# A weighted sum of two expert outputs: ten tiles of 13 or 12 tokens in place of eleven of 12 or 10

## The chip, the cores and the metric

The kernel runs on one core of one Trainium2 chip. The metric is the device time of one execution in microseconds (us); the median of three runs of the kernel before is 239.36 us (239.26 to 239.48). The core's VectorE (DVE), ScalarE (ACT) and SyncE (SP) are used; TensorE does nothing here and GpSimd (POOL) only sets a few constants. Data goes between the device's memory (HBM) and the core's on-chip memory (SBUF, 128 partitions) by DMA transfers, which SP and ACT issue from their own instruction streams, each into a queue of its own (q1 of the profile is SP's, q10 is ACT's). Sixteen DMA engines serve both queues.

## The reference

For each of 16 x 1024 = 16,384 tokens there are two rows of 512 float32 values (the outputs of two experts) and two weights; the result is the weighted sum of the two rows.

```python
def setup_inputs():
    batch, seq, hidden, n_experts, k = 16, 1024, 512, 8, 2
    return {
        "expert_outputs": np.random.randn(batch, seq, k, hidden).astype(np.float32),
        "combine_weights": np.random.randn(batch, seq, k).astype(np.float32),
    }

def reference(expert_outputs, combine_weights):
    weights = combine_weights[..., np.newaxis]
    return np.sum(expert_outputs * weights, axis=2).astype(np.float32)
```

So 64 MiB come in, 128 KiB of weights come in, and 32 MiB go out. There are 3 x 512 arithmetic operations a token.

## The kernel before

Each of the 128 partitions takes 128 tokens. One token is 4 KB of input (its two rows lie side by side) and 2 KB of output, so a tile of c tokens on all partitions is c x 512 KB of input, in 128 contiguous rows of c x 4 KB, one for a partition, and c x 256 KB of output, in 128 rows of c x 2 KB.

Which tokens belong to which partition is settled in two regions (`rows`, lines 40 to 44). The first `main` = 10 tokens of every partition come from the first 1,280 tokens of the input, and the other `LAST` = 118 from the rest. Inside a region a partition's tokens are contiguous, so from one partition's row to the next the input steps by 40 KB in the first region and by 118 x 4 KB = 472 KB in the second; the output steps by half of that.

The work is cut into 11 tiles (`TILES`, line 30) of 10, 12 (nine times) and 10 tokens. Four rooms of 12 tokens each lie in one SBUF tile, `et`; tile g is loaded into room g % 4, is worked on there in place, and its result is put into the first half of the same room. In what follows ln is the load of tile n, sn the store of its results, w0 the first transfer of weights and w1 the second.

The order on each engine is the order of the program (`tc.manual_schedule`); only waits for data hold an instruction up.

- SP issues the loads (`load`, line 71): first l0 in two transfers, of 2 and 8 tokens (the 2 tokens in pieces of 4 KB), and l1, l2 and l3. From then on l(g+4) is issued when sg has landed, because it overwrites the room that sg reads. SP also issues the last two stores.
- ACT issues, at the start, a small store of zeros ahead of everything (line 104, 16 pieces of 512 B, overwritten later by s0), then w0 (10 tokens' weights) and w1 (118 tokens' weights), and then the stores s0 to s6 (line 121).
- DVE multiplies a whole tile by its weights in one instruction (line 83), then adds its two halves in another (line 90). This holds for tiles 0 to 8 (`WHOLE`).
- Tile 9 (`MIXED`) shares the work: ACT multiplies the first expert's rows, one instruction a token (line 87), DVE the second expert's in one instruction (line 89), and DVE adds (line 90).
- Tile 10 goes token by token: ACT multiplies the first expert's row (line 95), DVE multiplies the second and adds the first (line 96).
- The results of tiles 7 and 8 leave as one store of 24 tokens (48 KB rows), those of tiles 9 and 10 as one of 22 tokens (44 KB rows); both stores are issued by SP.

Of the kernel before, what the change touches and what calls it, by code (L numbers as in the profile page):

```python
# [1 line left out]

# [4 lines left out]


@with_exitstack
def kernel(  # L10
    ctx: ExitStack,
    tc: tile.TileContext,
    expert_outputs: bass.AP,
    combine_weights: bass.AP,
    out: bass.AP,
):

    nc = tc.nc
    b, s, k, h = expert_outputs.shape
    assert k == 2
    n = b * s
    P = nc.NUM_PARTITIONS
    per = n // P
    assert per * P == n

    ROOM, ROOMS = 12, 4
    TILES = [10, 12, 12, 12, 12, 12, 12, 12, 12, 12, 10]  # L30
    FIRST = [2, 8, 12, 12, 12]
    STORES = [[0], [1], [2], [3], [4], [5], [6], [7, 8], [9, 10]]
    WHOLE = [0, 1, 2, 3, 4, 5, 6, 7, 8]
    MIXED = [9]
    LAST = 118
    assert sum(TILES) == per and [g for st in STORES for g in st] == list(range(len(TILES)))
    main = per - LAST
    starts = [sum(TILES[:g]) for g in range(len(TILES))]

    def rows(x):  # L40

        first = x[0 : P * main, :].rearrange("(p t) f -> p t f", p=P)
        second = x[P * main : n, :].rearrange("(p t) f -> p t f", p=P)
        return lambda t, c: first[:, t : t + c, :] if t < main else second[:, t - main : t - main + c, :]

    flat = out.rearrange("b s h -> (b s) h")
    eo = rows(expert_outputs.rearrange("b s k h -> (b s) (k h)"))
    cw = rows(combine_weights.rearrange("b s k -> (b s) k"))
    o = rows(flat)

    dt = mybir.dt.float32
    mult = mybir.AluOpType.mult
    add = mybir.AluOpType.add
    copy = mybir.ActivationFunctionType.Copy

    pool = ctx.enter_context(tc.tile_pool(name="all", bufs=1))
    et = pool.tile([P, ROOMS * ROOM, k * h], dt)
    halves = et.rearrange("p j (k h) -> p (j k) h", k=k)
    wt = pool.tile([P, per * k], dt)
    wk = wt.rearrange("p (t k) -> p t k", k=k)  # L60
    zt = pool.tile([16, 128], dt)
    warm = pool.tile([P, 1], dt)

    def place(t):
        g = max(g for g in range(len(TILES)) if starts[g] <= t)
        return g % ROOMS * ROOM + t - starts[g]

    def load(t, c, **kw):
        at = place(t)
        assert place(t + c - 1) == at + c - 1  # L70
        nc.sync.dma_start(out=et[:, at : at + c], in_=eo(t, c), **kw)  # L71

    def weights(q, t, c):
        q.dma_start(out=wk[:, t : t + c, :], in_=cw(t, c))

    def combine(g, base):
        at, c, t0 = g % ROOMS * ROOM, TILES[g], starts[g]
        if g in WHOLE or g in MIXED:
            room = halves[:, k * at : k * (at + c), :]
            x0, x1 = et[:, at : at + c, 0:h], et[:, at : at + c, h : 2 * h]  # L80
            if g in WHOLE:
                wb = wt[:, k * t0 : k * (t0 + c)].unsqueeze(2).to_broadcast([P, k * c, h])
                nc.vector.tensor_tensor(out=room, in0=room, in1=wb, op=mult)  # L83
            else:
                for i in range(c):
                    x = et[:, at + i, 0:h]
                    nc.scalar.activation(out=x, in_=x, func=copy, scale=wt[:, k * (t0 + i) : k * (t0 + i) + 1])  # L87
                w1 = wk[:, t0 : t0 + c, 1:2].to_broadcast([P, c, h])
                nc.vector.tensor_tensor(out=x1, in0=x1, in1=w1, op=mult)  # L89
            nc.vector.tensor_tensor(out=halves[:, base : base + c, :], in0=x0, in1=x1, op=add)  # L90
            return
        for i in range(c):
            t = k * (t0 + i)
            x0, x1 = halves[:, k * (at + i), :], halves[:, k * (at + i) + 1, :]
            nc.scalar.activation(out=x0, in_=x0, func=copy, scale=wt[:, t : t + 1])  # L95
            nc.vector.scalar_tensor_tensor(  # L96
                out=halves[:, base + i, :], in0=x1, scalar=wt[:, t + 1 : t + 2], in1=x0, op0=mult, op1=add
            )

    with tc.manual_schedule():  # L100
        nc.vector.memset(zt, 0.0)  # L101

        ahead = flat[0 : P * main, :].rearrange("(q t) h -> q (t h)", q=16)
        nc.scalar.dma_start(out=ahead[:, 0:128], in_=zt)  # L104
        weights(nc.scalar, 0, main)
        weights(nc.scalar, main, per - main)
        nc.scalar.activation(out=warm, in_=nc.const_aps.tensor(1.0, (P, 1), dt), func=copy)  # L107

        t = 0
        for i, c in enumerate(FIRST):  # L110
            load(t, c, **({"max_dma_last_dim": k * h * 4} if i == 0 else {}))
            t += c
        assert t == sum(TILES[:ROOMS])
        for j, st in enumerate(STORES):
            base, c = st[0] % ROOMS * ROOM * k, 0
            for g in st:
                combine(g, base + c)
                c += TILES[g]
            assert c <= k * ROOM
            q = nc.sync if j in (7, 8) else nc.scalar  # L120
            q.dma_start(out=o(starts[st[0]], c), in_=halves[:, base : base + c, :])
            for g in st:
                if g + ROOMS < len(TILES):
                    load(starts[g + ROOMS], TILES[g + ROOMS])


# [1 line left out]
_INS = ['expert_outputs', 'combine_weights']  # L128
_OUTS = [((16, 1024, 512), 'float32')]


# [23 lines left out]
```

## Time and profile before

| what | value |
|---|---|
| median of 3 runs | 239.36 us (239.26 to 239.48) |
| span of the profiled execution, first to last instruction | 237.6 us |
| what lies around the span, against the median | 1.8 us |
| DVE busy | 192.1 us (81%) |
| ACT busy | 15.2 us (6%) |
| moved by DMA | 100.80 MB, 424 GB/s over the span |
| loads and weights on SP's and ACT's queues, HBM read | 67.24 MB |
| HBM written | 33.56 MB |

The profiled execution has no device time of its own on record beside its span; the median of the runs stands in for it, so 237.6 us of span and 1.8 us around it make its 239.4 us.

The page's DMA line gives, in 40 slices of the span, the share of time in which the 16 DMA engines had a packet in hand, and the line below it what they moved. A window row gives the same for a stretch that is asked for; it counts a packet where it starts, so a short stretch is blurred by the packets at its edges. The list of DMA issues gives the time from the issue of a transfer to its landing, queueing included. The waits of SP are those of its queue of DMA issues, which is not counted as busy time.

### The profile page before, as it was taken

How to read it: one execution, taken by the hardware profiler on the slowest of the kernel's cores; microseconds unless marked ns; L12 is line 12 of the kernel's file. 1: busy time of each engine (PE TensorE's matmuls, PEld its weight loads, DVE VectorE, ACT ScalarE, POOL GpSimd, SP SyncE). 2: the span in 40 equal slices, each digit the busy share in tenths (PEclk: the TensorE clock that was granted, in tenths of full speed). 3: DMA queues.
4: the chain of work that ended last, by engine and by line, in shares of the span. 5: the costliest groups of instructions: out<-in, count | busy, mean ns of one | idle time of the engine just before them, and what ended most of it. 6: DMA issues, size and time to landing. Idle time of an engine off the chain costs nothing.

```text
span 237.6 us, 154 instructions
## 1 busy us (share of the span) xinstructions
DVE 192.1 (81%) x31; ACT 15.2 (6%) x24; POOL 0.2 (0%) x4
## 2 busy tenths in 40 slices
DVE  0039999999999996998799699969987999998000
ACT  2000000000000000000000000000000008482000
POOL 0000000000000000000000000000000000000000
DMA  7999998999999999999999999999999999999895
GB/s 266 442 445 405 456 481 375 375 430 477 439 447 414 397 405 455 463 397 430 430 505 422 447 414 397 414 447 463 397 439 422 463 404 434 441 463 463 375 485 243
DMA packets 3472, 100.80 MB, mean 424 GB/s; under 512 B 512, under 2 KB 656, under 8 KB 912
## 3 DMA queue, kind: packets, MB, share of 16 engines
q1 hardware_dynamic: 2144, 79.17, 77.6%
q10 hardware_dynamic: 1328, 21.64, 21.2%
HBM read 67.24 MB, written 33.56 MB: 424 GB/s over the span
## 4 chain that ended last, share of the span: by engine, by line
DMA 60%; DVE 30%; issue 1%; DVEq 0%; ACTq 0%; SPq 0%
DMA et<-in_expert_outputs_dram 30%; DMA out_dram<-et 24%; DVE et L83 15%; DVE et L90 10%; DMA wt<-in_combine_weights_dram 6%; DVE et L89 3%; DVE et L96 3%; DVEq L150 0%; ACTq L104 0%; DVE zt L101 0%; SPq L71 0%; DVEq L96 0%; DVEq L83 0%; DVEq L90 0%
## 5 line engine op out<-in xcount | busy, mean ns | idle before, releaser
L83 DVE TENSOR_TENSOR et<-et,wt 128x12288 f32<-128x12288 f32 (+1 forms) x9 | 114.5, 12719 | 25.8 <-DMA wt<-in_combine_weights_dram 14.9
L90 DVE TENSOR_TENSOR et<-et 128x6144 f32<-128x6144 f32 (+1 forms) x10 | 64.5, 6451 | 0.4
L87 ACT ACTIVATE et<-et,wt 128x512 f32<-128x512 f32 x12 | 7.5, 709 | 193.0 <-DMA et<-in_expert_outputs_dram 193.0
L96 DVE SCALAR_TENSOR_TENSOR et<-et,wt 128x512 f32<-128x512 f32 x10 | 6.7, 747 | 0.1
L89 DVE TENSOR_TENSOR et<-et,wt 128x6144 f32<-128x6144 f32 x1 | 6.6, 6552 | 0.0
L95 ACT ACTIVATE et<-et,wt 128x512 f32<-128x512 f32 x10 | 6.2, 707 | 4.7 <-DMA et<-in_expert_outputs_dram 4.7
L107 ACT ACT_TABLE_LOAD x1 | 1.3, 1283 | 2.4 <-issue 2.4
L101 DVE MEMSET zt<- 16x128 f32 x1 | 0.2, 165 | 0.8 <-PEq L139 0.8
L107 ACT ACTIVATE warm<-const-float32-1.0 128x1 f32<-128x1 f32 x1 | 0.2, 203 | 0.0
L139 POOL MEMSET const-bfloat16-1.0<- 128x1 bf16 x1 | 0.1, 101 | 0.0
L139 POOL MEMSET const-uint8-127<- 128x1 uint8 x1 | 0.1, 101 | 0.0
L139 POOL MEMSET const-float32-0.0<- 128x1 f32 x1 | 0.1, 98 | 0.2 <-issue 0.2
L139 POOL MEMSET const-float32-1.0<- 128x1 f32 x1 | 0.1, 98 | 0.0
## 6 DMA issues: line engine op xcount, KB each, us to landing
et<-in_expert_outputs_dram SPq DMA_DIRECT2D x9, 6144.0 KB, 35.3
out_dram<-et ACTq DMA_DIRECT2D x6, 3072.0 KB, 31.9
out_dram<-et SPq DMA_DIRECT2D x1, 6144.0 KB, 24.3
out_dram<-et SPq DMA_DIRECT2D x1, 5632.0 KB, 17.6
et<-in_expert_outputs_dram SPq DMA_DIRECT2D x1, 5120.0 KB, 21.1
et<-in_expert_outputs_dram SPq DMA_DIRECT2D x1, 4096.0 KB, 14.4
out_dram<-et ACTq DMA_DIRECT2D x1, 2560.0 KB, 24.9
et<-in_expert_outputs_dram SPq DMA_DIRECT2D x1, 1024.0 KB, 5.1
```

What stands on the lines that cost most here:

```text
L83: nc.vector.tensor_tensor(out=room, in0=room, in1=wb, op=mult)
L87: nc.scalar.activation(out=x, in_=x, func=copy, scale=wt[:, k * (t0 + i) : k * (t0 + i) + 1])
L89: nc.vector.tensor_tensor(out=x1, in0=x1, in1=w1, op=mult)
L90: nc.vector.tensor_tensor(out=halves[:, base : base + c, :], in0=x0, in1=x1, op=add)
L95: nc.scalar.activation(out=x0, in_=x0, func=copy, scale=wt[:, t : t + 1])
L96: nc.vector.scalar_tensor_tensor(out=halves[:, base + i, :], in0=x1, scalar=wt[:, t + 1 : t + 2], in1=x0, op0=mult, op1=add)
L101: nc.vector.memset(zt, 0.0)
L107: nc.scalar.activation(out=warm, in_=nc.const_aps.tensor(1.0, (P, 1), dt), func=copy)
L139: nc = _bacc.Bacc("TRN2", target_bir_lowering=False, num_devices=1)
```

## The change

The four rooms hold 13, 13, 12 and 13 tokens, and there are ten tiles, of 13 tokens, except tiles 2 and 6, which have 12 and share the room of 12. The first 115 tokens of each partition make the first region (460 KB from one partition's input row to the next, 230 KB in the output), and the last 13, which are tile 9, the second (52 KB and 26 KB).

- l0 comes as 2 and 11 tokens; the other loads are whole tiles. SP issues 11 loads in place of 12, and again the last two stores.
- The weights come in three transfers in place of two, on ACT's queue: 13 tokens (w0), 102 tokens (w1), and 13 tokens for tile 9 (w2), which lie in the second region.
- Tiles 0 to 7 are done as whole tiles. Tile 8 is the mixed one: DVE multiplies the first expert's rows of its first 3 tokens in an instruction of its own, ACT those of the other 10, and DVE the second expert's rows of all 13, then adds. Tile 9 goes token by token on ACT and DVE (`pair`).
- The results of tiles 7 and 8 leave as one store of 26 tokens (52 KB rows). The results of tile 9 leave alone (26 KB rows); they are put into the room of 12, which held tile 6, and its own room is only read.

```diff
-    ROOM, ROOMS = 12, 4
-    TILES = [10, 12, 12, 12, 12, 12, 12, 12, 12, 12, 10]
-    FIRST = [2, 8, 12, 12, 12]
-    STORES = [[0], [1], [2], [3], [4], [5], [6], [7, 8], [9, 10]]
-    WHOLE = [0, 1, 2, 3, 4, 5, 6, 7, 8]
-    MIXED = [9]
-    LAST = 118
+    SIZES = [13, 13, 12, 13]
+    ROOMS = len(SIZES)
+    ROOM0 = [sum(SIZES[:r]) for r in range(ROOMS)]
+    TILES = [13, 13, 12, 13, 13, 13, 12, 13, 13, 13]
+    FIRST = [2, 11, 13, 12, 13]
+    STORES = [[0], [1], [2], [3], [4], [5], [6], [7, 8], [9]]
+    MIXED = {8: 3}
+    LAST = 115
+    N = len(TILES)
...
-        first = x[0 : P * main, :].rearrange("(p t) f -> p t f", p=P)
-        second = x[P * main : n, :].rearrange("(p t) f -> p t f", p=P)
+        first = x[0 : P * LAST, :].rearrange("(p t) f -> p t f", p=P)
+        second = x[P * LAST : n, :].rearrange("(p t) f -> p t f", p=P)
...
+        if g == N - 1:
+            for i in range(c):
+                pair(t0 + i, x0[:, i, :], x1[:, i, :], halves[:, base + i, :])
             return
...
+        if g in MIXED:
+            v = MIXED[g]
+            for i in range(v, c):
+                x = x0[:, i, :]
+                nc.scalar.activation(out=x, in_=x, func=copy, scale=wt[:, k * (t0 + i) : k * (t0 + i) + 1])
+            w0 = wk[:, t0 : t0 + v, 0:1].to_broadcast([P, v, h])
+            nc.vector.tensor_tensor(out=x0[:, 0:v, :], in0=x0[:, 0:v, :], in1=w0, op=mult)
+            w1 = wk[:, t0 : t0 + c, 1:2].to_broadcast([P, c, h])
+            nc.vector.tensor_tensor(out=x1, in0=x1, in1=w1, op=mult)
...
-        weights(nc.scalar, 0, main)
-        weights(nc.scalar, main, per - main)
+        weights(nc.scalar, 0, TILES[0])
+        weights(nc.scalar, TILES[0], LAST - TILES[0])
+        weights(nc.scalar, LAST, per - LAST)
...
+        load(0, 0, 2, max_dma_last_dim=k * h * 4)
+        load(0, 2)
+        for g in range(1, ROOMS):
+            load(g)
         for j, st in enumerate(STORES):
-            base, c = st[0] % ROOMS * ROOM * k, 0
+            base = k * ROOM0[st[0] % ROOMS if st != [N - 1] else (N - 4) % ROOMS]
+            c = 0
```

More of the change, by code (lines that the diff above doesn't have):

```diff
@@ L27 @@
     assert per * P == n
-    ROOM, ROOMS = 12, 4
-    TILES = [10, 12, 12, 12, 12, 12, 12, 12, 12, 12, 10]
-    FIRST = [2, 8, 12, 12, 12]
-    STORES = [[0], [1], [2], [3], [4], [5], [6], [7, 8], [9, 10]]
-    WHOLE = [0, 1, 2, 3, 4, 5, 6, 7, 8]
-    MIXED = [9]
-    LAST = 118
-    assert sum(TILES) == per and [g for st in STORES for g in st] == list(range(len(TILES)))
-    main = per - LAST
-    starts = [sum(TILES[:g]) for g in range(len(TILES))]
+    SIZES = [13, 13, 12, 13]
[7 more added lines that the diff above has]
+    N = len(TILES)
+    assert sum(TILES) == per
+    starts = [sum(TILES[:g]) for g in range(N)]
     def rows(x):
-        first = x[0 : P * main, :].rearrange("(p t) f -> p t f", p=P)
-        second = x[P * main : n, :].rearrange("(p t) f -> p t f", p=P)
-        return lambda t, c: first[:, t : t + c, :] if t < main else second[:, t - main : t - main + c, :]
+        first = x[0 : P * LAST, :].rearrange("(p t) f -> p t f", p=P)
+        second = x[P * LAST : n, :].rearrange("(p t) f -> p t f", p=P)
+        return lambda t, c: first[:, t : t + c, :] if t < LAST else second[:, t - LAST : t - LAST + c, :]
     flat = out.rearrange("b s h -> (b s) h")
@@ L56 @@
     pool = ctx.enter_context(tc.tile_pool(name="all", bufs=1))
-    et = pool.tile([P, ROOMS * ROOM, k * h], dt)
+    et = pool.tile([P, sum(SIZES), k * h], dt)
     halves = et.rearrange("p j (k h) -> p (j k) h", k=k)
@@ L62, with load @@
     warm = pool.tile([P, 1], dt)
[L64 to L71, printed above, removed]
+    def load(g, skip=0, c=None, **kw):
+        c = TILES[g] - skip if c is None else c
+        at = ROOM0[g % ROOMS] + skip
+        nc.sync.dma_start(out=et[:, at : at + c], in_=eo(starts[g] + skip, c), **kw)
@@ L73, in weights @@
     def weights(q, t, c):
         q.dma_start(out=wk[:, t : t + c, :], in_=cw(t, c))
-    def combine(g, base):
[L77 to L90, printed above, removed]
-            return
[L92 to L98, printed above, removed]
@@ new lines, in pair @@
+    def pair(t, x0, x1, y):
+        nc.scalar.activation(out=x0, in_=x0, func=copy, scale=wt[:, k * t : k * t + 1])
+        nc.vector.scalar_tensor_tensor(
+            out=y, in0=x1, scalar=wt[:, k * t + 1 : k * t + 2], in1=x0, op0=mult, op1=add
+        )
+    def combine(g, base):
+        at, c, t0 = ROOM0[g % ROOMS], TILES[g], starts[g]
+        room = halves[:, k * at : k * (at + c), :]
+        x0, x1 = et[:, at : at + c, 0:h], et[:, at : at + c, h : 2 * h]
+        if g == N - 1:
+            for i in range(c):
+                pair(t0 + i, x0[:, i, :], x1[:, i, :], halves[:, base + i, :])
+            return
+        if g in MIXED:
[7 more added lines that the diff above has]
+            nc.vector.tensor_tensor(out=x1, in0=x1, in1=w1, op=mult)
+        else:
+            wb = wt[:, k * t0 : k * (t0 + c)].unsqueeze(2).to_broadcast([P, k * c, h])
+            nc.vector.tensor_tensor(out=room, in0=room, in1=wb, op=mult)
+        nc.vector.tensor_tensor(out=halves[:, base : base + c, :], in0=x0, in1=x1, op=add)
@@ L100 @@
     with tc.manual_schedule():
         nc.vector.memset(zt, 0.0)
-        ahead = flat[0 : P * main, :].rearrange("(q t) h -> q (t h)", q=16)
+        ahead = flat[0 : P * LAST, :].rearrange("(q t) h -> q (t h)", q=16)
         nc.scalar.dma_start(out=ahead[:, 0:128], in_=zt)
-        weights(nc.scalar, 0, main)
-        weights(nc.scalar, main, per - main)
+        weights(nc.scalar, 0, TILES[0])
+        weights(nc.scalar, TILES[0], LAST - TILES[0])
+        weights(nc.scalar, LAST, per - LAST)
@@ L107 @@
         nc.scalar.activation(out=warm, in_=nc.const_aps.tensor(1.0, (P, 1), dt), func=copy)
[L109 to L113, printed above, removed]
+        load(0, 0, 2, max_dma_last_dim=k * h * 4)
+        load(0, 2)
+        for g in range(1, ROOMS):
+            load(g)
         for j, st in enumerate(STORES):
-            base, c = st[0] % ROOMS * ROOM * k, 0
+            base = k * ROOM0[st[0] % ROOMS if st != [N - 1] else (N - 4) % ROOMS]
+            c = 0
@@ L118 @@
                 c += TILES[g]
-            assert c <= k * ROOM
             q = nc.sync if j in (7, 8) else nc.scalar
@@ L122 @@
             for g in st:
-                if g + ROOMS < len(TILES):
-                    load(starts[g + ROOMS], TILES[g + ROOMS])
+                if g + ROOMS < N:
+                    load(g + ROOMS)
 _INS = ['expert_outputs', 'combine_weights']
```

## The prediction

> **What bounds the kernel now.** I read the page's DMA lines first, then the rate in windows cut at the landings of loads, then SP's waits, the forms of instructions, and at last the issues of transfers one by one.
>
> ```profile
> span 237.6 us, 154 instructions
> ...
> DVE 192.1 (81%) x31; ACT 15.2 (6%) x24; POOL 0.2 (0%) x4
> ...
> DMA  7999998999999999999999999999999999999895
> ...
> DMA packets 3472, 100.80 MB, mean 424 GB/s; under 512 B 512, under 2 KB 656, under 8 KB 912
> ```
>
> ```profile
> core 0: us, DVE busy (x) ACT busy (x) POOL busy (x), PEclk, DMA share, GB/s
> 0.00:1.80 1.80, 0.17 (x1) 0.00 (x0) 0.20 (x4) 1.00 0.00 0
> 15.66:30.58 14.92, 14.63 (x2) 0.00 (x0) 0.00 (x0) 1.00 1.00 430
> 30.58:70.79 40.21, 40.14 (x5) 0.00 (x0) 0.00 (x0) 1.00 0.99 418
> 92.57:179.65 87.08, 78.06 (x8) 0.00 (x0) 0.00 (x0) 1.00 1.00 434
> ```
>
> ```profile
> SPq L71 <- DMA out_dram<-et: 169.7, 7, 41.5
> ```
>
> The DMA engines are full from the first slice to the last but one. The windows say at what rate: 430 GB/s where l1 runs with w1 alone, 434 where loads and stores alternate. 100.80 MB at 434 GB/s are 232.3 us. Before the first byte lie 1.80 us (the first window), and after the last landing, at 236.8 as worked out below, 0.8 us of span. These make 234.9 of 237.6 us. Of the 2.7 us left, the window from 30.58 to 70.79 holds most: at 418 rather than 434 GB/s it loses 40.21 x (1 - 418/434) = 1.5 us, blurred by the packets at its edges. DVE is 81% busy, but its idle time and SP's 169.7 us of waits for stores are the same thing seen twice: loads wait for rooms, and rooms for stores that share the DMA engines. So bytes decide, as long as some transfer is always queued. The change moves the same bytes. It can act only through holes in the DMA, through the cost of a row or an alternation, and through the two ends.
>
> **The two ends and the first tiles.** These rows carry the schedule: issue to landing, and the times of issue.
>
> ```profile
> et<-in_expert_outputs_dram SPq DMA_DIRECT2D x1, 4096.0 KB, 14.4
> et<-in_expert_outputs_dram SPq DMA_DIRECT2D x1, 1024.0 KB, 5.1
> ```
>
> ```profile
> et<-in_expert_outputs_dram SPq DMA_DIRECT2D x1, 6144.0 KB, 28.9
> wt<-in_combine_weights_dram ACTq DMA_DIRECT2D x1, 118.0 KB, 28.9
> wt<-in_combine_weights_dram ACTq DMA_DIRECT2D x1, 10.0 KB, 14.4
> ```
>
> ```profile
> 15.92 10.83 DVE L83 TENSOR_TENSOR et<-et,wt 128x10240 f32<-128x10240 f32 x1 [14.94 <-DMA wt<-in_combine_weights_dram]
> ...
> 212.45 6.71 DVE L96 SCALAR_TENSOR_TENSOR et<-et,wt 128x512 f32<-128x512 f32 x10
> ```
>
> ```profile
> 32.30 0.35 ACTq L121 DMA_DIRECT2D out_dram<-et  x1
> ```
>
> ```profile
> 187.86 0.33 SPq L71 DMA_DIRECT2D et<-in_expert_outputs_dram  x1
> ```
>
> ```profile
> 219.19 0.34 SPq L121 DMA_DIRECT2D out_dram<-et  x1
> ```
>
> ```profile
> 199.25 20.28 SPq L121 DMA_DIRECT2D out_dram<-et  x2
> ```
>
> ```profile
> out_dram<-et SPq DMA_DIRECT2D x1, 6144.0 KB, 24.3
> out_dram<-et SPq DMA_DIRECT2D x1, 5632.0 KB, 17.6
> et<-in_expert_outputs_dram SPq DMA_DIRECT2D x1, 5120.0 KB, 21.1
> ```
>
> The last load lands at 187.86 + 21.1 = 209.0. The first of the two closing stores goes out at 199.25 and lands at 199.25 + 24.3 = 223.5, the second at 219.19 and lands at 219.19 + 17.6 = 236.8. Between these two landings 5632 KB (5.767 MB) take 13.24 us, 435 GB/s with stores alone: no hole, though the second store was issued only 223.5 - 219.2 = 4.3 us before the first had landed. That lead is the yardstick below.
>
> w1, with one row for each partition, landed 28.9 us after issue, just as long as l1 of as many rows. So the two queues take turns row by row, whatever the rows' size.
>
> **The change part by part, and its cost.** Durations for the compute come from here:
>
> ```profile
> L83 DVE TENSOR_TENSOR et<-et,wt 128x12288 f32<-128x12288 f32 x8 | 103.6, 12956 | 10.8 <-DMA et<-in_expert_outputs_dram 10.8
> L90 DVE TENSOR_TENSOR et<-et 128x6144 f32<-128x6144 f32 x9 | 59.0, 6558 | 0.4
> L87 ACT ACTIVATE et<-et,wt 128x512 f32<-128x512 f32 x12 | 7.5, 709 | 193.0 <-DMA et<-in_expert_outputs_dram 193.0
> ...
> L89 DVE TENSOR_TENSOR et<-et,wt 128x6144 f32<-128x6144 f32 x1 | 6.6, 6552 | 0.0
> ```
>
> *First tile larger (13 tokens).* l0's second part grows by 3 tokens, 1.57 MB or 3.7 us at 430 GB/s, so l0 and w0 land near 19.4 in place of 15.7 us. Tile 0 then takes DVE 13/12 x (12.96 + 6.56) = 21.1 us, and s0 goes out at 40.5 in place of 32.3. Cost: nothing, because four rooms now hold 51 tokens (26.7 MB) in place of 46, and that load alone keeps the engines busy past 61 us. From there the first stores carry on. Uncovered, the 3.7 us would count in full.
>
> *w2, a third transfer of weights.* The bytes of weights are the same 128 KB. New are 8 more rows a DMA engine, each taking a turn against a row of l2. A price for turns with such small rows: l1 with w1 is 6.412 MB, 14.73 us at the 435 GB/s of stores alone; it took 14.92, 0.19 us more. A price for turns of loads with stores: one load and one store, 9.437 MB, take 21.77 us (the 87.08 us window holds four) against 21.68 at 435: 0.09 us for 8 turns. The bounds are 0 (if the 0.19 us belong to l1 alone) and +0.2; I take +0.1, as the price in the row that mixes loads and stores and near the middle. In ACT's queue s0 stands behind w2, which lasts as long as l2, to about 51 us. So s0 starts some 8 us later than its issue, and lands near l3, at about 74 us; only then can l4 go out. At that moment SP's queue runs dry, and the DMA lives from s1 alone, issued at 40.5 + 21.1 = 61.6, with 3328 KB or 7.8 us of work. That is the cover. l4 needs only the 1.1 us that l0 needed from its issue (0.7) to the first byte (1.80). Without the cover these 1.1 us would be lost.
>
> The Trainium skill, "DMA: Bandwidth & Descriptors", section "Queues, rings and completion order", has each DMA engine change between queues only after a packet of some 9 to 17 descriptors. By that rule w2's eight rows would pass in one turn, s0 would not be held by l2, and the hole at 74 us would not even need its cover; the sum would lose the +0.1 us. The trace does not agree: w1, landing with l1 after 28.9 us, took its turns one row at a time.
>
> *One load less, rows of 52 in place of 48 KB.* SP saves one issue of 0.33 us, off the path, since SP waits 169.7 us for stores. Each engine has 8 load rows fewer; if the 0.19 us of the l1 window were the load rows' own, that would be worth up to -0.2 us. The stores s0 to s6 are seven as before, with 56 rows an engine and as many turns against loads. I take 0, bounds -0.2 and 0, since stores and loads together run within 0.4% of stores alone.
>
> *Other pitch.* The two regions of before have 40 and 472 KB. l0's second part with w0 (4106 KB from 5.8, where the 1024 KB landed, to 1.2 + 14.4 = 15.6 us) makes about 429 GB/s at 40 KB pitch, and l1 430 GB/s at 472 KB. I take 0 for 460 KB and for 52 KB; what it would cost is a rival.
>
> *The tail.* After l9 lands, what is left is s7 with s8, 6656 KB, and s9, 3328 KB: 10.22 MB at 435 GB/s, 23.5 us. With an end at 236.9, l9 lands at 213.4. l8 lands before it by l9's 6656 KB and by what is left of s6 then, some 2100 KB: 8.97 MB at 434 GB/s, so at 192.7. Tile 8 costs DVE 1536 elements, 13 x 512 and again 13 x 512, at 6552/6144 ns each: 1.6 + 7.1 + 7.1 = 15.8 us; ACT's 10 rows at 0.709 us run beside it. The store of tiles 7 and 8 goes out at 208.5, 4.9 us before l9 has landed, where 4.3 us was enough before. Tile 9: one ACT row, 0.7 us, then 13 x 0.671 = 8.7 us on DVE (212.45 row: 6.71 us for 10), so s9 goes out at 222.8; the store before it lands at 236.9 - 7.8 = 229.1, a lead of 6.3 us. Its results go to tile 6's room, whose store lands before 210: no wait. Lanes of completion semaphores used again (by l3, from the store of zeros) are free within 6 us. Cost 0.
>
> *DVE's work.* Tiles 0 to 7 hold 102 tokens at 1.626 us, 165.9; with 15.8 and 8.7 that is 190.4 against 192.1 us. Off the path, nothing.
>
> The sum: 237.6 + 0.1 = 237.7 us of span, and with the 1.8 us around it (the median of the runs, 239.36, less 237.6) 239.45 us. Its own bounds, -0.2 to +0.2 for each of two terms, give 239.1 to 239.8.
>
> **Rivals.** *Slower, a hole before the closing stores.* If the store of tiles 7 and 8 comes too late to follow l9, the DMA is idle once l9 is through. For: its lead of 4.9 us rests on an estimate of what is left of s6, and each engine sits on a row of l9 for 52 KB / 27.2 GB/s = 1.96 us. It decides where the lead falls under that row and the 1.1 us from issue to first byte, about 3 us. Against: 4.3 us sufficed before. Price: up to 1.1 us, or the 1.96 us of a row if DVE is late by that much: 240.6 to 241.4; I put it at 240.9.
>
> *Faster, the early loss goes.* The window 30.58 to 70.79 loses up to 1.5 us, at no wait that the profile shows; it is where the first store joins the loads, and the change moves that moment by 8 us. Were half of it gone, 0.75 us: 238.7. Against: the cause isn't visible, and the first store still has to join.
>
> *Slower, the pitch.* If 460 KB spreads worse over memory than 472 KB, 1% of the loads' 67 MB at 434 GB/s is 1.5 us: 241.0. Against: 40 KB and 472 KB run alike here.
>
> [...]
>
> **How the numbers follow.** My forecast, no change that can be measured, has 0.60; the early loss going 0.16; the hole 0.13; the pitch 0.07; other losses near the start 0.04. About 0.2% (0.5 us) is what a measurement of this kernel tells from no change. Faster by more: 0.16; within: 0.60; slower: 0.24. The predicted time is 239.45, with 239.1 to 239.8 as that case's own range. For 8 in 10 I reach to half the early loss and to the near end of the hole, with a little on the fast side: 238.6 to 240.6.
>
> **What would show it.** Steps right: windows of alternating loads and stores still at 434 GB/s; first multiply near 19.4; first large store issued near 40.5, and landing near 74 with SP's l4 just after it; the 26-token store issued 4 to 5 us before l9 lands; the last store issued near 222.8; DMA slices without a digit under 8 but at the ends. Wrong: a window of low rate near 74 or 213 (a hole), steady windows below 430 (pitch), or a window at 30 to 75 us at 430 or more (the early loss gone).

## The result, and the profile after

The changed kernel takes 240.71 us (median of four runs, 240.34 to 240.81), the one before 239.42 us in the same comparison: a ratio of 1.0054, with a 95% interval of 1.0040 to 1.0068. It is 1.3 us slower, where 239.45 us and no measurable change had been forecast, and just outside the range.

The page of the changed kernel, its lines on the span, DVE and the DMA:

```profile
span 239.0 us, 155 instructions
...
DVE 190.2 (80%) x33; ACT 15.8 (7%) x25; POOL 0.2 (0%) x4
...
DMA  7989999999999999999999999999999999989995
...
DMA packets 3472, 100.80 MB, mean 422 GB/s; under 512 B 640, under 2 KB 784, under 8 KB 1040
```

The same bytes, the same full DMA line, and 1.4 us more of span. So the engines were hardly ever without a packet, but somewhere a packet took longer. Windows of the changed kernel, cut at the landings of l0, l1, l3, l4 and l8, with one more for 77 to 85.2 us:

```profile
core 0: us, DVE busy (x) ACT busy (x) POOL busy (x), PEclk, DMA share, GB/s
0.00:1.80 1.80, 0.17 (x1) 0.00 (x0) 0.20 (x4) 1.00 0.00 0
19.02:34.98 15.96, 15.84 (x2) 0.00 (x0) 0.00 (x0) 1.00 1.00 429
34.98:73.74 38.76, 38.73 (x4) 0.00 (x0) 0.00 (x0) 1.00 0.98 417
73.74:103.70 29.96, 28.04 (x4) 0.00 (x0) 0.00 (x0) 1.00 1.02 426
77.00:85.20 8.20, 8.20 (x2) 0.00 (x0) 0.00 (x0) 1.00 0.99 367
103.70:196.20 92.50, 82.87 (x8) 0.00 (x0) 0.00 (x0) 1.00 1.00 434
```

Loads alone run at 429 and the steady part at 434 GB/s, as before. New is the stretch from 77 to 85 us: 367 GB/s with a DMA share of 0.99. The kernel before has a low figure there too, but with a lower share, and the two go together where packets are counted at their starts:

```profile
77.00:85.00 8.00, 7.97 (x2) 0.00 (x0) 0.00 (x0) 1.00 0.91 393
```

393 GB/s at a share of 0.91 are 432 for a full share, as in the steady part; 367 at 0.99 are only 371. The stretch belongs to what happened at 74 us, which these rows of the changed kernel show (from issue to landing for w2 and s0; times of issue for s0, l4 and the two closing stores):

```profile
wt<-in_combine_weights_dram ACTq DMA_DIRECT2D x1, 13.0 KB, 47.4
...
40.29 0.35 ACTq L122 DMA_DIRECT2D out_dram<-et  x1
...
out_dram<-et ACTq DMA_DIRECT2D x1, 3328.0 KB, 33.6
...
73.97 0.33 SPq L68 DMA_DIRECT2D et<-in_expert_outputs_dram  x1
...
212.28 0.35 SPq L122 DMA_DIRECT2D out_dram<-et  x1
...
224.21 0.34 SPq L122 DMA_DIRECT2D out_dram<-et  x1
```

s0 goes out at 40.29 and lands at 40.29 + 33.6 = 73.9, with l3 (73.74); l4 is issued at 73.97 into an empty queue. (In these rows wt is w2, 40.29 is s0, 73.97 is l4, 212.28 and 224.21 are the closing stores of 26 and of 13 tokens.)

A window counts a packet where it starts. For the rest I spread each packet of the trace evenly over its own time and asked how far the bytes moved lag behind a steady 435.2 GB/s, a yardstick near the 435 GB/s of the last store before. The lag in us at eight moments, for the profiled executions of the two kernels and six of the experiments (told below). At 236 us f4 and h1 have moved all their bytes, so their 4.37 there is only the end of the count:

```
us from start              6     30     40     60     75     85    200    236
before                  2.77   2.96   3.31   3.89   3.95   3.99   4.44   4.57
changed                 2.49   2.67   2.76   3.52   3.58   4.85   5.30   5.53
two transfers (f4)      2.51   2.66   2.72   3.39   3.44   3.48   3.92   4.37
hold put back (g2)      2.51   2.66   2.74   3.28   3.35   4.65   5.09   5.27
hold, swapped (g3)      2.61   2.76   2.87   3.31   3.37   4.72   5.16   5.36
l4 late (h1)            2.48   2.62   2.68   3.40   3.45   3.50   3.93   4.37
two ahead of s0 (e4)    2.49   2.66   2.73   2.92   3.92   3.96   4.39   4.53
before with w2 (e2)     2.72   2.93   3.02   3.21   3.67   4.05   4.51   4.62
```

The changed kernel starts 0.28 us better, is still 0.37 us ahead at 75 us, loses 1.27 us in the ten that follow, and then keeps pace. At 236 us it is 0.96 us behind; the last 0.5 us of the span lie at the end: the 16 engines complete the last store between 237.15 and 238.22 us, before the change between 236.22 and 236.77.

The packets of the changed kernel show the join of l4 (load rows of 53,248 B, store rows of 26,624 B; grouped by order of start, durations are means):

```
store rows 75.93..76.33 x16, 987 ns each
store rows 76.92..77.31 x16, 1049 ns
store rows 77.90..78.20 x12, 1184 ns
load rows  78.31..79.68 x15, 2709 ns    (1966 ns in the steady part)
...
completions of s1, one for each engine: 87.86 to 90.92
```

Four engines took l4's first row a turn before the other twelve; rows of both kinds went slow (the longest load row took 3246 ns), and from then on the engines were up to 3 us apart. Engines without a packet account for little of it: between 73.5 and 91 us all sixteen together lack 1.55 us, 0.1 us for each.

### The profile page after: what moved, and what is told of

Same layout as the page of the kernel before. It is cut to its first block, busy times and chain, and to the rows that moved or that the text cites. A ratio compares the mean times of both kernels' runs of the same rounds, so it can differ in the third digit from the quotient of the medians.

```text
span 239.0 us, 155 instructions
## 1 busy us (share of the span) xinstructions
DVE 190.2 (80%) x33; ACT 15.8 (7%) x25; POOL 0.2 (0%) x4
## 4 chain that ended last, share of the span: by engine, by line
DMA 63%; DVE 28%; issue 2%; ACT 0%; DVEq 0%; ACTq 0%; SPq 0%
DMA et<-in_expert_outputs_dram 28%; DMA out_dram<-et 27%; DVE et L98 18%; DMA wt<-in_combine_weights_dram 7%; DVE et L99 7%; DVE et L75 3%; ACT et L74 0%; DVEq L151 0%; ACTq L105 0%; DVE zt L102 0%; DVEq L98 0%; SPq L68 0%; ACTq L74 0%
## 5 line engine op out<-in xcount | busy, mean ns | idle before, releaser
L98 DVE TENSOR_TENSOR et<-et,wt 128x13312 f32<-128x13312 f32 (+1 forms) x8 | 110.1, 13756 | 27.5 <-DMA wt<-in_combine_weights_dram 18.1
L99 DVE TENSOR_TENSOR et<-et 128x6656 f32<-128x6656 f32 (+1 forms) x9 | 62.8, 6973 | 0.4
L91 ACT ACTIVATE et<-et,wt 128x512 f32<-128x512 f32 x10 | 6.2, 712 | 191.8 <-DMA et<-in_expert_outputs_dram 191.8
L75 DVE SCALAR_TENSOR_TENSOR et<-et,wt 128x512 f32<-128x512 f32 x13 | 8.7, 747 | 3.2 <-ACT et L74 3.2
L74 ACT ACTIVATE et<-et,wt 128x512 f32<-128x512 f32 x13 | 8.1, 713 | 12.2 <-DMA et<-in_expert_outputs_dram 12.2
L95 DVE TENSOR_TENSOR et<-et,wt 128x6656 f32<-128x6656 f32 x1 | 7.1, 7084 | 0.0
L93 DVE TENSOR_TENSOR et<-et,wt 128x1536 f32<-128x1536 f32 x1 | 1.8, 1759 | 2.1 <-DMA et<-in_expert_outputs_dram 2.1
```

Source lines behind the costliest of these rows:

```text
L75: nc.vector.scalar_tensor_tensor(out=y, in0=x1, scalar=wt[:, k * t + 1 : k * t + 2], in1=x0, op0=mult, op1=add)
L93: nc.vector.tensor_tensor(out=x0[:, 0:v, :], in0=x0[:, 0:v, :], in1=w0, op=mult)
```

## The experiments

Two theories stood first. A: w2, which takes its turns row by row beside l2, holds s0 back; s0 lands with l3, the load queue runs dry, and the late join of l4 costs the time. B: the rows of 52 KB, or the pitch of 460 KB, cost it.

**e1: w2 behind l3 on SP's queue.**

```diff
-        weights(nc.scalar, LAST, per - LAST)
...
             load(g)
+        weights(nc.sync, LAST, per - LAST)
```

> The changed kernel with one edit: w2 is issued by SP behind l3, no longer by ACT ahead of s0. Theory A (w2, row by row behind l2, holds s0 back; s0 lands with l3, SP's queue runs dry, and the joining of l4 at 77 to 85 us slows all engines by 1.2 us and leaves them 1 us apart at the end): s0 starts near 44 us and lands near 66 to 68, l4 is issued before l3 lands, the slow stretch at 77 to 85 us is gone, and the time falls from 240.7 by 1.2 to 1.7 us, to 239.0 to 239.5. Theory B (the rows of 52 KB or the pitch of 460 KB cost it): 240.5 to 240.9, and a slow stretch stays.

Measured: 243.81 us, ratio 1.0179 (1.0151 to 1.0206). s0 did land early, at 67.7, and l4 was issued at 67.76. But on SP's queue w2 stood ahead of l4, and each of its rows of 104 B waited for a row of s1 of 0.98 us, so l4 began only at 80.8 us. A slow stretch of 0.57 us followed when s2 joined at 83 to 91, the engines drifted apart until l8 landed between 195.9 and 200.2, and DVE, which needs all of l8, issued the store of 26 tokens at 216.33, when l9 was through:

```profile
212.50:217.00 4.50, 3.80 (x1) 0.06 (x1) 0.00 (x0) 1.00 0.11 47
```

47 GB/s for 4.5 us is the hole that the prediction had as a rival. The time missed both expectations; the experiment moved the hold from s0 to l4 and so decides neither theory.

**e2: a w2 in the kernel before.**

```diff
-        weights(nc.scalar, main, per - main)
+        weights(nc.scalar, main, 105)
+        weights(nc.scalar, main + 105, 13)
```

> The kernel before with one edit: w1's 118 tokens come in two transfers on ACT's queue, of 105 and of 13, so that 8 more rows for each engine stand ahead of s0. Theory A: s0 starts only when l2 is through (about 49 us), lands with l3 near 71, SP's queue runs dry, l4 joins late; 0.8 to 1.7 us slower than before, 240.2 to 241.1. Theory B: 0.0 to 0.2 us slower, 239.4 to 239.6.

Measured: 239.58 us, ratio 1.0007 (0.9997 to 1.0017). The schedule came out as A says: s0 landed at 66.0 with l3 at 65.8, and l4 joined at 69.7 to 70.8, six engines a turn ahead of ten. The price did not, and the time lies in the range of B: the table shows 0.84 us lost from 60 to 85, but at 60 us the kernel was 0.68 us ahead, since the stumble that costs the kernel before 0.5 us at 45 to 48 us is missing here.

**e3: the regions swapped, and so no w2.**

```diff
-        first = x[0 : P * LAST, :].rearrange("(p t) f -> p t f", p=P)
+        first = x[0 : P * HEAD, :].rearrange("(p t) f -> p t f", p=P)
...
+        weights(nc.scalar, 0, HEAD)
+        weights(nc.scalar, HEAD, per - HEAD)
```

with `HEAD = 13` in place of `LAST` throughout.

> The changed kernel with the regions the other way round: the first 13 tokens of each partition are the first region (52 KB pitch), the other 115 the second (460 KB). Two transfers of weights do (13 and 115 tokens), there is no w2. Theory A: as with w2 on SP's queue, 239.0 to 239.5; if the faster start of the changed kernel (0.28 us) came from the pitch of its first rows, it is lost here and this kernel lies 0.3 us above that one. Theory B (the pitch of 460 KB): 240.5 to 240.9.

Measured: 238.98 us, ratio 0.9985 (0.9975 to 0.9996): the same tiles, rooms, rows of 52 KB and pitch of 460 KB, a little faster than before, with 0.04 us lost from 75 to 85. B is out. The lag at 6 us is 2.67 us, between the 2.77 of before and the 2.49 of the changed kernel.

**e4: two small transfers ahead of s0.**

```diff
-        weights(nc.scalar, TILES[0], LAST - TILES[0])
+        weights(nc.scalar, TILES[0], 51)
+        weights(nc.scalar, TILES[0] + 51, 51)
```

> The changed kernel with w1 cut into two transfers of 51 tokens, so that two small transfers stand ahead of s0 and beside l2 and l3. Theory A with a fixed price of a queue that runs dry and is joined again: 240.5 to 241.0, the slow stretch moved later (s0 starts near 66 us and lands near 75 to 82). If the price grows with how long SP's queue is dry: 241.0 to 243. Theory B: 240.7 to 241.0, and the slow stretch stays at 77 to 85 us.

Measured: 239.30 us, ratio 0.9996 (0.9987 to 1.0006). All of the expectations missed. s0 waited until l3 was nearly through (66 us), the load queue ran dry for 12 us, and at 77.7 to 78.6 l4, issued at 74.21, joined without loss: 15 of 16 engines took its first row in one step, at 1966 ns a row. So a dry queue has no fixed price. The issue of l4:

```profile
74.21 0.33 SPq L68 DMA_DIRECT2D et<-in_expert_outputs_dram  x1
```

This made the second theory, A2: the join costs, by how its moment falls among the engines. Its rival C: the 13-token rooms lose the time whatever w2 does.

**f1: w2 behind s6. f4: the first region's weights in one transfer, so that two stand ahead of s0, as before the change.**

```diff
-        weights(nc.scalar, LAST, per - LAST)
...
+            if j == 6:
+                weights(nc.scalar, LAST, per - LAST)
```

```diff
-        weights(nc.scalar, 0, TILES[0])
-        weights(nc.scalar, TILES[0], LAST - TILES[0])
+        weights(nc.scalar, 0, LAST)
         weights(nc.scalar, LAST, per - LAST)
```

> The changed kernel with w2 issued by ACT behind s6, where nothing waits behind it. Theory A2 (the loss of the changed kernel lies where the loads, having run dry because w2 held s0 back, join the running store again: rows go slow there and the engines part; the moment of the join among the engines decides how much, 0 to 1.3 us): s0 lands near 68, l4 is issued before l3 lands, no slow stretch at 77 to 85 us, the last landings within 0.6 us of each other, 238.7 to 239.2. Theory C (13-token rooms lose it whatever w2 does, and the swapped regions cured it by the pitch of tile 4's rows): a slow stretch at 75 to 90 us of 0.5 us or more, 239.8 to 240.9.

> The changed kernel with the weights of the first region, 115 tokens, in one transfer, so that only two transfers stand ahead of s0, as before the change, and s0 joins beside l2. Theory A2: as with w2 last, 238.7 to 239.3. Theory C: 239.8 to 240.9.

f4 took 238.95 us, ratio 0.9982 (0.9971 to 0.9993), with no slow stretch. Its windows from l3's landing to l4's, and on to l8's, and the issues of l4 and of the store of 26 tokens:

```profile
76.55:99.94 23.39, 23.36 (x3) 0.00 (x0) 0.00 (x0) 1.00 1.00 431
99.94:192.47 92.53, 84.98 (x9) 0.00 (x0) 0.00 (x0) 1.00 1.00 433
...
67.74 0.33 SPq L68 DMA_DIRECT2D et<-in_expert_outputs_dram  x1
...
208.47 0.35 SPq L121 DMA_DIRECT2D out_dram<-et  x1
```

f1 took 243.98 us, ratio 1.0195 (1.0178 to 1.0212), outside both ranges, but lost nothing at 77 to 85 (at 200 us its lag was 3.97 us, f4's 3.92). Near the end w2's rows took turns with rows of the closing store and landed at 222.5; ACT waited for them, and the last store landed 5 us later than f4's. From the waits of f1:

```profile
ACT et L74 <- DMA wt<-in_combine_weights_dram: 24.0, 1, 24.0
```

C falls, and A2 stands so far; f1's own loss is the same row-by-row turn at a place where I had not reckoned with it.

**f5: the room of 12 second.** The edit was wrong: tile 9 with its 13 tokens then shares the room of 12, and overwrites a token of the next one, which chains the tiles. 292.43 us say nothing on the question.

```diff
-    SIZES = [13, 13, 12, 13]
+    SIZES = [13, 12, 13, 13]
...
-    TILES = [13, 13, 12, 13, 13, 13, 12, 13, 13, 13]
+    TILES = [13, 12, 13, 13, 13, 12, 13, 13, 13, 13]
```

> The changed kernel with the room of 12 second in place of third (rooms of 13, 12, 13, 13; w2 still ahead of s0). The hold and the dry queue stay, only the moment of the join moves against the engines' rows. Theory A2: s0 still lands with l3, and the loss at the join lies anywhere from 0 to 1.3 us: 239.0 to 240.8. If the loss of a dry queue were a fixed price: 240.5 to 240.9. Theory C: 240.5 to 240.9.

**f6: the kernel before with a long pitch at the start.**

```diff
-    LAST = 118
+    LAST = 22
```

> The kernel before with its first region of 106 tokens (424 KB from row to row) and the last 22 tokens, the last store's, as the second region; the weights come as 106 and 22 tokens. If the faster start of the changed kernel (0.28 us in the first 6 us) comes from a long pitch of the first rows: 0.2 to 0.4 us faster than before, 238.9 to 239.1. If it has another cause: 239.2 to 239.5.

Measured: 239.22 us, ratio 0.9996 (0.9986 to 1.0005). The lag at 6 us fell from 2.77 to 2.53 us, as in the changed kernel; the time did not follow beyond its uncertainty and lies in the range of "another cause"; in the profiled run the stumble at 45 to 48 us was 0.2 us larger.

**g2 and g3: the hold put back, into f4 and into e3.**

```diff
-        weights(nc.scalar, LAST, per - LAST)
+        weights(nc.scalar, LAST, 7)
+        weights(nc.scalar, LAST + 7, per - LAST - 7)
```

```diff
-        weights(nc.scalar, HEAD, per - HEAD)
+        weights(nc.scalar, HEAD, 102)
+        weights(nc.scalar, HEAD + 102, 13)
```

> The kernel with two transfers of weights (115 and 13 tokens) and one edit: the 13 tokens come as 7 and 6, so that again a third small transfer stands ahead of s0, beside l2. Theory A2: s0 waits until l2 is through, lands with l3 near 74, the loads run dry and join late; a slow stretch comes back between 72 and 90 us, 239.3 to 240.8 against 238.95 without the third transfer. If the third transfer does nothing: 238.9 to 239.1.

> The kernel with the regions swapped and the second region's 115 tokens of weights cut into 102 and 13: the hold put back in another layout. Theory A2: as above, 239.3 to 240.8 against 238.98 without it. If the third transfer does nothing: 238.9 to 239.1.

Measured: 240.50 us (1.0050, 1.0035 to 1.0065) and 240.56 us (1.0053, 1.0038 to 1.0068), 1.55 and 1.58 us more than without the third transfer. Both show the changed kernel's picture: s0 landing at 73.7, six and five engines taking l4's first row a turn ahead of the others, a loss of 1.30 and 1.35 us from 75 to 85, engines 1 us apart at the end. From g2, the issue of l4 and the window from l3's landing to l4's:

```profile
73.71 0.33 SPq L68 DMA_DIRECT2D et<-in_expert_outputs_dram  x1
...
73.48:103.54 30.06, 28.59 (x4) 0.00 (x0) 0.00 (x0) 1.00 1.02 424
```

So one more transfer of 128 small rows ahead of s0 costs 1.5 to 1.8 us in three kernels with the new tiles, whatever its bytes (6 KB in g2, 13 KB in the others). It is no rule: with the old tiles (e2) it cost 0.3 us, and with one more still (e4) 0.35 us over f4.

**g4 and g5: the load queue dry without the hold, first try.** DVE was to clear part of tile 0's free room after it had multiplied tile 2, so that l4 would be late. I had put the clearing behind l4 in the program; so DVE waited for l4 instead, and cleared what it had loaded (one value a partition in g4, half a token in g5).

```diff
             nc.vector.tensor_tensor(out=room, in0=room, in1=wb, op=mult)
+            if g == 2:
+                nc.vector.memset(et[:, 12, h : h + 1], 0.0)
```

> The kernel with two transfers of weights; DVE clears one column of tile 0's free room right after it has multiplied tile 2, so l4, which overwrites that room, is issued near 74.7 in place of 67.7 us, while s0 starts and lands as early as without it. The loads run dry near 76.5 and join s1 near 78.6. If the dry queue and its late join cost the time: a slow stretch after 78 us, 239.2 to 240.3. If the late s0 costs it, and not the dry queue: 238.9 to 239.1.

> The same with 512 columns cleared in place of one, so l4 joins some 0.3 to 0.6 us later against the stores' rows of 0.98 us. If the price of the join hangs on the moment: another loss than with one column, anywhere from 0 to 1.3 us (238.95 to 240.3). If the price is fixed: the same as with one column to 0.2 us.

251.10 and 251.63 us, and nothing follows for the question. The waits and the timeline of g4 show why; l4 landed at 97.2 us, and DVE cleared only then:

```profile
DVE et L101 <- issue: 22.5, 1, 22.5
...
97.22 0.06 DVE L100 MEMSET et<- 128x1 f32 x1
```

**h1 to h5: the same with l4 behind the clearing in the program.** The kernel is f4; l4 and l5 are issued after the clearing, which is all that differs between the five: 1 column (h1), 512 (h2), 912 (h4), 420 (h5), and in h3 one column after DVE has added tile 2.

```diff
+    def late(cols):
+        nc.vector.memset(et[:, 12, h : h + cols], 0.0)
+        load(4)
+        load(5)
...
             nc.vector.tensor_tensor(out=room, in0=room, in1=wb, op=mult)
+            if g == 2:
+                late(1)
```

> The kernel with two transfers of weights; DVE clears one column of tile 0's free room right after it has multiplied tile 2, and l4, which overwrites that room and now stands behind that in the program, is issued near 74.7 in place of 67.7 us. s0 starts and lands as early as without it. The loads run dry near 76.5 and join s1 near 78.6. If the dry queue and its late join cost the time: a slow stretch after 78 us and engines apart, 239.2 to 240.6. If the late start of s0 costs it, and not the dry queue: 238.9 to 239.1.

> The same with 512 columns cleared in place of one, so l4 joins some 0.3 to 0.6 us later against the stores' rows of 0.98 us. If the price of the join hangs on the moment: another loss than with one column, 0 to 1.3 us. If it is fixed: the same as with one column to 0.2 us.

> The same, one column, cleared after DVE has added tile 2, so l4 is issued near 81.3 us and joins near 85, when s1 is about through and s2 begins. If the dry queue costs by its length: 1 us or more over the kernel with l4 at 74.7. If the join costs once, by its moment: 239.0 to 240.6, as with the two others. Later loads shorten the lead of the closing store of 26 tokens; a hole there would come on top.

h1: 238.94 us (ten runs, 238.84 to 239.02). l3's last rows ended at 74.9 to 75.2 (it landed at 76.5), four store rows passed alone, and all 16 engines took l4's first row in one step at 78.79 to 79.09, at 1969 ns. No loss (table), no drift. Its issue of l4, and the window from l3's landing to l4's:

```profile
74.53 0.33 SPq L68 DMA_DIRECT2D et<-in_expert_outputs_dram  x1
...
76.50:101.67 25.17, 25.14 (x3) 0.00 (x0) 0.00 (x0) 1.00 1.00 432
```

By its own expectation h1 speaks against the dry queue, and for the late start of s0 as the cause. Against that stands e4: its s0 began at 65 to 66 us, the changed kernel's at 51.4, and yet l4 joined without loss. What the changed kernel, g2 and g3 have in common, against h1, e4 (but for one engine) and f4, is the join out of step; e2 has it too, at a smaller loss (0.38 us from 75 to 85).

h2: 239.33 us, but its ten runs lie between 238.95 and 240.84. l4 is issued at 75.09, and the engines begin their next store row at 74.96 to 75.38. In h1 the issue fell 0.3 us ahead of such a turn.

h3: 243.41 us, ratio 1.0164 (1.0147 to 1.0182). Here l4 came when s1 was through as well: no row in flight from 81.1 to 82.1 us, 2.7 us lost there, the engines up to 4 us apart, and so a hole of 3.3 us before the closing store. With both queues empty it does not tell the length of the dry time from the moment of the join.

That made a prediction to test: an issue between two turns costs nothing, one on a turn scatters.

> The kernel with l4 late, with 912 columns cleared in place of 512 (in two instructions), so l4 is issued near 75.5 us, in the middle of a store row (rows turn near 75.0 to 75.4 and 75.9 to 76.4). If what decides is whether the issue falls on the turn of the rows: all runs within 0.3 us of each other, 238.9 to 239.2, and the profile shows all 16 engines taking l4's first row in one step. If half a row more or less says nothing: runs scattered as with 512 columns (238.95 to 240.84).

> The same with 420 columns, so l4 is issued near 75.0 us, on the turn of the rows. If the turn decides: runs scattered over 1 us or more, or all near 240.3 to 240.8, and the median above 239.1. If not: 238.9 to 239.1, as with one column.

h4, issue at 75.44 between the turns: 238.93 us, ten runs within 238.89 to 239.01. h5, issue at 75.03 on the turn: 239.53 us, ten runs from 238.89 to 240.23, six of them above 239.4. Both as expected. (The kernel before has 5 of 93 runs between 240.2 and 240.6 too, so a single long run says little.) The rows of issue, h2, h4 and h5 in this order:

```profile
75.09 0.33 SPq L68 DMA_DIRECT2D et<-in_expert_outputs_dram  x1
```

```profile
75.44 0.33 SPq L68 DMA_DIRECT2D et<-in_expert_outputs_dram  x1
```

```profile
75.03 0.33 SPq L68 DMA_DIRECT2D et<-in_expert_outputs_dram  x1
```

In the profiled executions of h2 and h5 (239.05 and 238.89 us) the engines joined in step; no long one was profiled, so that their long runs joined out of step is argued, not seen. The profiles agree with it: issued between 74.53 and 75.09, h1, h2 and h5 have l4's first rows in the same turn (78.8 to 79.3), and h4, issued at 75.44, a turn later (79.8 to 80.1), so what decides between two turns lies there between 75.09 and 75.44, close behind the issues that scatter.

In the changed kernel, g2 and g3 the issue of l4 follows the completion of s0, which is itself a turn in s0's queue (72.97 to 73.37 in the changed kernel), by 0.6 to 1.0 us, where a store row takes 0.99, and so falls on or just ahead of the next turn (73.97, with turns at 73.96 to 74.36; 73.71 with 73.78 to 74.11 in g2; 73.74 with 73.83 to 74.12 in g3). e4 is an exception: its issue at 74.21 also falls on a turn (74.22 to 74.78), one engine was out of step, and its ten runs lie within 239.18 to 239.44. So an issue on a turn can cost up to 1.9 us (h2's spread), and need not. Why it scatters in h2 and h5, costs nothing in e4 and costs in every run of the changed kernel, g2 and g3, and why the rows go slow when the engines split, stays open.

**What it amounts to.** f4 is the change without its loss: 238.95 us against 239.32 for the kernel before in the same comparison, 0.18% faster (0.07% to 0.29%); h4 reads 0.9977 (0.9964 to 0.9990).

## Why the prediction was wrong, point by point

*That bytes decide and the steady part stays*: right. 434 GB/s before and after, loads alone 430 and 429.

*First tile larger, cost nothing*: right. The first multiply starts at 19.11 (19.4 forecast), s0 goes out at 40.29 (40.5).

*The sum's own range*: the terms' bounds, 0 to +0.2 and -0.2 to 0, give 239.2 to 239.6, not 239.1 to 239.8; the measured time lies outside both.

*w2, the step that failed.* Its mechanism up to 74 us came as written: s0 stood behind w2, landed at 73.9 with l3, and l4 went out at 73.97 into a dry queue. The failure is in the next sentence, that s1's 7.8 us of work is the cover and only 1.1 us would be lost without it. The cover was there, and the engines lacked packets for no more than 0.1 us. But l4's first row began 4.3 us after its issue, not 1.1 us (that alone cost nothing: h1 has the same 4.3); four engines took it ahead of the others, rows went slow, and 1.27 us were lost under full cover; and the engines, apart from then on, ended 0.5 us later. I had treated bytes in the queue as the only thing that a join could cost. The term was +0.1 us with a bound of +0.2; f4 against the changed kernel makes it 1.76 us, g2 and g3 1.55 and 1.58.

*The rule on turns*: by the Trainium skill, "DMA: Bandwidth & Descriptors", section "Queues, rings and completion order", w2 would have passed in one turn of 9 to 17 descriptors, and s0 would not have been held. The changed kernel's w2, 13 KB in 8 rows an engine, took 47.4 us to land, with l2; e1 and f1 show the same beside stores. The measurement decides: one row a turn, here. The same page, section "Why a DMA increments its semaphore by 16 and not by 1", says that the engines of one transfer finish independently and only the full count means that all has landed. There the trace agrees: s1's completions spread over 3.1 us, and every load and DVE tile behind such a landing waits for the last engine. In the steady part that cost nothing (434 GB/s); at the end, where the last store's completions are 1.1 us apart in place of 0.55 before, it did.

*One load less, rows of 52 KB, cost 0*: right as far as f4 can tell; its steady lag grows by 0.44 us from 85 to 200, before by 0.45.

*Other pitch, cost 0*: a gain of about 0.25 us in the first 6 us was missed; f6, which has it alone, did not get measurably faster. The first rows start faster at 460 KB or 424 KB (lag at 6 us 2.49 and 2.53) than at 40 KB (2.77), with 52 KB between (2.67).

*The tail, cost 0*: right for f4, where l8 landed at 192.5 (192.7 forecast), the store of 26 tokens went out at 208.47 (208.5) and led l9's landing at 212.6 by 4.1 us (4.9). In the changed kernel the loss and the drift made l8 land at 196.2, the store went out at 212.28, and the lead over l9 at 214.6 was 2.3 us; 0.1 us was lost there.

*The rivals*: the hole before the closing store hardly came in the changed kernel, but e1, f1 and h3 have it, at 3.3 to 5.1 us, more than the 1.1 to 1.96 us that I allowed. The early loss did not go: 0.99 us between 30 and 75 us before, 0.91 after, 0.78 in f4. The pitch did no harm.

## What to carry to other kernels

Where two queues share the DMA engines row by row, as here, a transfer of a few KB holds whatever stands behind it for as many of the other queue's rows as it has rows itself: count its rows, not its bytes, and keep it out of the way of the first store and of the last wait. A queue that runs dry beside a full one can be paid for even though hardly an engine idles, so look at when each queue is joined again, and not only at whether any work is left. A small change whose runs scatter, like h2's, is worth a second place half a row away.

## What the runs showed of the hardware that was not expected

- The first row of a transfer began 1.1 us after issue on idle engines (0.73 to 1.81 us), but 3.5 us (l4 in e4), 4.3 us (l4 in the changed kernel and h1) and 4.8 us (s0 before the change, 32.30 to 37.1) where the other queue kept them busy.
- At a join, load rows took 2709 ns on average and up to 3246 ns, against 1966 ns. Where the first store joins, the lag grew by 0.35 us in the kernel before (30 to 40 us), 0.67 us in f4 (40 to 60) and 1.00 us in e4 (60 to 75); the kernel before stumbled a second time by 0.5 us at 45 to 48 us with no instruction starting a transfer near it.
- Engines that are out of step stay so: 3 us apart at 88 us in the changed kernel, still 1.1 us at the last store, while the rate stays at 434 GB/s.
- A transfer's completion takes a turn in its queue as well: s0's last data row began at 53.7 to 54.3 in the kernel before, and its completions came after the next load row, at 56.3 to 56.8.
